# Four of the second layer's six conditioning vectors formed by VectorE sums during the first mixer, and the softmax reciprocals' products placed behind a score block's first transposes

## The chip, the cores and the metric

The kernel runs on one core of a Trainium2 chip, in float32. The metric is device time in microseconds of a whole execution. The kernel before took 1665.06 us in the median of three runs (1663.93 to 1668.5).

Engines are named as in the profile: PE (matrix products), DVE (vector), ACT (scalar, table functions), POOL (general), SP (issues DMAs). A queue is the list of DMAs that one engine issues in order.

## The reference

A two-layer backbone over 512 latent tokens and 256 context tokens, width 1024. Each layer: conditioning, a mixer, an expert layer. Layer 0 mixes by Fourier groups and a short gated convolution; layer 1 by windowed attention with four key heads. Cut to what the change touches:

```python
def reference(...):
    for layer in range(2):
        mod_l = silu(c) @ w_mod[layer] + b_mod[layer]        # 6 vectors of 1024, latent tokens
        mod_c = silu(c_ctx) @ w_mod[layer] + b_mod[layer]    # the same, context tokens
        sh1_l, sc1_l, g1_l, sh2_l, sc2_l, g2_l = split(mod_l, 6)
        sh1_c, sc1_c, g1_c, sh2_c, sc2_c, g2_c = split(mod_c, 6)
        hl = modulate(rms_norm(xl, norm_mix_g[layer]), sh1_l, sc1_l)   # vectors 0 and 1
        ...                                  # mixer; layer 1 makes no output for the context tokens
        xl = xl + g1_l * yl                                            # vector 2
        hl2 = modulate(rms_norm(xl, norm_ffn_g[layer]), sh2_l, sc2_l)  # vectors 3 and 4
        if last:
            xl = xl + g2_l * hier_moe(hl2, ...)                        # vector 5
```

In the last layer the context tokens need only vectors 0 and 1. In the attention, the weights of one query are exp(score - max) over their sum; the kernel multiplies by the reciprocal of that sum at the end.

## The kernel before, in words

**Stages.** Start and norm to 40 us; first mixer (input projection, four Fourier groups, four convolution groups) to 227; output projection and router of layer 0, `mixer_out`, to 326; experts of layer 0 to 830, which stream the experts' weights; keys, values and queries of layer 1 to 953; score blocks to 1100; `mixer_out` of layer 1 to 1157; experts of layer 1 to the end.

**Conditioning vectors.** `ModFeed` makes two vectors at a time (a group), for latent and context tokens at once, in four steps. A step takes a 2 MB piece of `w_mod` in a slot of a shared ring, multiplies it on PE by the silu of the conditioning (`sil`, 32 columns, eight float32 products of 512 columns, line 1035) and has DVE add the sum to the bias (line 1040); POOL stores the finished group in a scratch tensor in device memory, `mod_d` (line 1043). Groups 0 to 2 of layer 0 and group 0 of layer 1 are made in the first mixer: there the loads are issued by POOL (line 1013), each when PE has finished with the slot that it re-uses. Groups 1 and 2 of layer 1 are made in the attention layer, where SP issues the loads: two steps among the key and value blocks, one at the end of each of the first six score blocks.

**First mixer.** PE multiplies weights that are split into a high part (`whi`, by ACT) and a rest (`wlo`, by DVE, line 1206) by the normalized tokens: 24 pairs of a 512- and a 256-column product per group of 128 channels (lines 1210 and 1211). Four groups go through a discrete Fourier transform (lines 1227, 1250 and 1253, with DVE's butterflies into `Z` between), four through the convolution.

**Score blocks.** Eight blocks, each of eight heads by 128 queries. In block n PE makes the scores of block n, one or two heads at a time (line 1783; DVE adds the mask and finds the maximum, ACT takes exp, line 1789), and between them transposes the weights of block n-1 (`pv_tile`, line 1830) and multiplies them by the values (`pv_mm`, line 1845). At the end `pv_end` spreads the reciprocals `es` of block n-1 over the 64 rows of a head by 16 small products by the identity (line 1856), ACT copies them to SBUF (line 1858), DVE multiplies.

**What sets the order.** Outside stretches marked `in_order` a scheduler with a timeline of its own places the instructions of each engine; each engine then runs its list in that order and waits where a value is missing. PE's order in the score blocks and in `mixer_out` is the written one. SP's and POOL's queues run in their listed order too.

**mixer_out.** It needs the rows of `mod_d` that layer 0's group 1 and 2 hold: `md` (line 1325) for the router's products on PE (line 1331), `gr`, `a`, `h` and `b` (line 1337) for gates and norms. SP loads them all, after the six 512 KB tiles of `x` (line 1432), and before the experts' first weights `w` and `r` (line 721).

Of the kernel before, what the change touches and what calls it, by code (L numbers as in the profile page):

```python
# [10 lines left out]
F32 = mybir.dt.float32  # L11
# [9 lines left out]
D = 1024  # L21
# [64 lines left out]
def body(tc, I, out, upto=None, dbg=None):  # L86
# [29 lines left out]
    def close(*ps):  # L116
        for p in ps:
            p_close.pop(id(p)).__exit__(None, None, None)
# [23 lines left out]
    one_ = stat.tile([128, 1], BF, name="one_")  # L142
    V.memset(one_, 1.0)
    ones = one_.to_broadcast([128, 128])
    epst = stat.tile([128, 1], F32, name="epst")
    V.memset(epst, EPS)
    rsq = stat.tile([128, 2, 4], F32, name="rsq")
# [849 lines left out]
    class ModFeed:  # L997
# [20 lines left out]
        def step(self, again=-1):  # L1018
# [22 lines left out]
            if q == 3:  # L1041
                for s in range(2):
                    G.dma_start(mod_d[l, s, g * 2048:(g + 1) * 2048].rearrange("(q n) -> q n", q=4), bm[s:128:32, :])


    xsrc = [I["x"][0, m * 128:(m + 1) * 128, :] for m in range(4)] + [I["ctx"][0, m * 128:(m + 1) * 128, :] for m in range(2)]
    pp = pool("ps0", space=PSUM)
# [107 lines left out]
    def put_y(g, pieces):  # L1155
        if len(ym) == 2:
            ym.append(R1a.tile([128, 2, 8, 256], F32R, name="r2"))
        for i, v in enumerate(pieces):
            S.copy(ym[i][:, 0, g, :], v)
            V.tensor_sub(ym[i][:, 1, g, :], v, ym[i][:, 0, g, :].bitcast(F32))  # L1160

    tp = pool("ptmp")
    cw = tp.tile([128, 3, 4], F32, name="cw")
    for t in range(3):
# [55 lines left out]
    def four_b(g, aT):  # L1220

        U = fp.tile([128, 6, 256], F32, name="U")
        for mm in range(3):
            p = psB([128, 2, 256])
            for i in range(2):
                m = 2 * mm + i
                T.matmul(p[:, i, :], aT[:, m * 128:(m + 1) * 128], dch, start=True, stop=True)
            S.copy(U[:, 2 * mm:2 * mm + 2, :], p)
        sm = U[:, 0:2, :]
        df = fp.tile([128, 2, 256], F32, name="df")  # L1230
        Z = fp.tile([128, 6, 2, 128], F32, name="Z")
        V.tensor_sub(df, U[:, 0:2, :], U[:, 2:4, :])
        V.tensor_add(sm, U[:, 0:2, :], U[:, 2:4, :])

        def zf(e):
            return Z[:, e].rearrange("p a c -> p (a c)")

        V.tensor_add(zf(0), sm[:, 0], sm[:, 1])
        V.tensor_sub(zf(2), sm[:, 0], sm[:, 1])
        C0, S0, C1, S1 = df[:, 0, 0:128], df[:, 0, 128:], df[:, 1, 0:128], df[:, 1, 128:]  # L1240
        V.tensor_sub(Z[:, 1, 0], C0, S1)
        V.tensor_add(Z[:, 1, 1], S0, C1)
        V.tensor_add(Z[:, 3, 0], C0, S1)
        V.tensor_sub(Z[:, 3, 1], S0, C1)
# [12 lines left out]
    load_conv(0)  # L1257
    pre = proj_pre()
    for g in range(4):
        aT = four_a(g)  # L1260
        if g:
            with tc.issue_after(mm["last"].ins):
                feed.step()
        if prev is not None:
            four_b(g - 1, prev)
        feed.step()
        prev = aT
    wo = I["w_out_even"][0].rearrange("(j p) d -> p j d", p=128)

# [7 lines left out]
    for j in range(4):  # L1277
# [10 lines left out]
        csb = tp.tile([128, L + LC + 4], F32, name="t3", bufs=2)  # L1288
        S.copy(csb[:, 0:L + LC], pc)
        feed.step()  # L1290
        load_conv(j + 1)
        if j == 3:
            wout = load_wout(0, 1)
# [5 lines left out]
        V.scalar_tensor_tensor(z[:, 1:1 + N2], u[:, 0:N2], cw[:, 0, j:j + 1], z[:, 1:1 + N2], op0=ALU.mult, op1=ALU.add)  # L1299
        V.scalar_tensor_tensor(z[:, 1:1 + N2], u[:, 2:2 + N2], cw[:, 2, j:j + 1], z[:, 1:1 + N2], op0=ALU.mult, op1=ALU.add)  # L1300
        feed.step()
        pb = proj(lambda k0: wr4[:, k0:k0 + 4, 0, :])
# [4 lines left out]
    close(cp, tp, hp)  # L1307


    def mixer_out(layer, NT, lhs, raws, whl, x1, psA, psB, hq, rq, mk_route, h2dst, mdp):  # L1310
# [256 lines left out]
    def cps(shape):  # L1567
        return mps.tile(shape, F32, name="cp", bufs=2)
# [14 lines left out]
    run(rest0)  # L1583

    feed = ModFeed([(1, 1), (1, 2)], lambda: cps([128, 512]), False)
    feed.load(0)
    close(mps, R1b, R1a, mp)
    pp = pool("ps1", space=PSUM)  # L1590
    kvp = pool("kvp")
# [111 lines left out]
            S.copy(kS[part][0:64, :, ms], p)  # L1703
            (V.tensor_copy)(kS[part][64:128, :, ms], p)

    feed.psum_tile = lambda: psB([128, 512])
    raw0 = load_qkv(0, 3)
    for i in range(8):
        if i == 4:
# [3 lines left out]
        for f, d in ((st_norm, 0), (st_kv, 1), (st_kt, 3)):  # L1713
            if 0 <= i - d < (4 if f is st_kt else 6):
                f(i - d)
        if i == 0:
            feed.step()
        if i == 2:
            feed.step(None)
    close(cb)  # L1720

    qS = []
# [79 lines left out]

    ohi, olo = [hpl.tile([128, 8, L], F32R, name=n) for n in ("hhi", "hlo")]
    av = slot(1, [128, 8, 512])
    feed.load(2)
    def s_end(n):
        G_ = n // 4
        nm, ls = st_[n][1:3]
# [39 lines left out]
    def pv_end(n):  # L1848

        G_, b = divmod(n, 4)  # L1850
        po, es = st_[n][3:5]
# [5 lines left out]
        o = av[:, 4 + n % 2]  # L1857
        S.copy(o, p.rearrange("p i q -> p (i q)"))
# [7 lines left out]
    with in_order(mybir.EngineType.PE):  # L1866
        for n in range(1, 9):
            if n < 8:
                s_begin(n)
            for i in range(5):  # L1870
# [2 lines left out]
                    s_head(n, c)  # L1873
                if n == 1 and i < 2:
                    st_qt(1, 2 + i)
                if n > 0:
                    pv_tile(n - 1, i)
                    pv_mm(n - 1, i - 1)
            if n > 0:
                pv_mm(n - 1, 4)  # L1880
                pv_end(n - 1)
            if n < 7:
                feed.step()
            if n < 8:
                s_end(n)
    close(wp, ro, ap_, kvp, fdp)
# [72 lines left out]
```

## Time and profile before

| | |
|---|---|
| median of three runs | 1665.06 us (1663.93 to 1668.5) |
| profiled execution, its own time | 1659.86 us |
| span of its trace | 1658.0 us |
| PE busy | 1530.3 us, 92% of the span |
| DVE, ACT, POOL busy | 723.6, 440.3, 124.4 us |
| device memory read | 499.31 MB |

The span is the time from the first to the last instruction that the trace holds; the execution's own time is 1.86 us longer. The profile lists busy time per engine, a table of stretches, the chain of work that ended last, and, for each engine, what ended its idle times. An engine's idle time matters only where that chain passes through it.

### The profile page before, as it was taken

What the parts mean: (1) busy time and instruction counts of PE and PEld (TensorE: products, weight loads), DVE (VectorE), ACT (ScalarE), POOL (GpSimd) and SP (SyncE); (2) the same over time, 40 slices, a digit from 0 to 9 for tenths busy, and PEclk for the clock granted to TensorE, in tenths of its full rate; (3) what the DMA queues carried; (4) which work ended last, traced back from release to release, by engine and by line L of the source; (5) the groups of instructions that cost most, each with busy time, mean ns of one, the idle gap of its engine ahead of it and who ended that gap; (6) DMA issues with size and microseconds to landing.
All of it is one profiled execution on the core that took longest, in us unless ns stands there. A gap on an engine that the chain in (4) does not pass through costs nothing.

```text
span 1658.0 us, 21618 instructions
## 1 busy us (share of the span) xinstructions
PE 1530.3 (92%) x8123; PEld 863.6 (52%) x8123; DVE 723.6 (44%) x1638; ACT 440.3 (27%) x879; POOL 124.4 (8%) x128
## 2 busy tenths in 40 slices
PE   5999989889999999999989989899899999976887
PEld 3677878734444444434447865678444445431332
DVE  3532435963425343433468965546522323310223
ACT  4321212211111011111065665544322222210110
POOL 2520001300000000000032300000000000000000
PEclk9999999989999999999999999999899999998999
DMA  9775353879999999999931024372699999999996
GB/s 372 277 294 169 111 180 108 288 303 419 419 419 402 383 420 418 419 419 419 359 137 51 1 102 154 112 174 95 271 419 421 419 420 420 420 420 420 420 420 252
DMA packets 106399, 503.53 MB, mean 304 GB/s; under 512 B 18384, under 2 KB 33232, under 8 KB 52272
## 3 DMA queue, kind: packets, MB, share of 16 engines
q1 hardware_dynamic: 95776, 464.09, 70.8%
q0 software_dynamic: 7344, 34.81, 5.5%
q10 hardware_dynamic: 3168, 3.17, 0.6%
q8 instruction: 67, 1.10, 0.3%
q14 instruction: 44, 0.36, 0.1%
HBM read 499.31 MB, written 5.34 MB: 304 GB/s over the span
## 4 chain that ended last, share of the span: by engine, by line
PE 34%; DMA 10%; DVE 3%; ACT 3%; issue 1%; SPq 0%; ACTq 0%; DVEq 0%
PE p L860 9%; DMA hhi<-in_w_dram 5%; PE yp L931 5%; DMA w<-in_w_dram 4%; PE cp L809 3%; PE A L1378 3%; PE tp L765 3%; PE A L1660 2%; PE A L1783 2%; PE O L1845 2%; PE B L1830 2%; DMA r<-in_w_dram 1%; PE B L1035 1%; ACT P L1789 1%; PE tp L772 1%
## 5 line engine op out<-in xcount | busy, mean ns | idle before, releaser
L860 PE MATMUL p<-w,xt 128*64 128x512 f32 (+1 forms) x1024 | 339.5, 618 | 16.7 <-DMA w<-in_w_dram 16.6
L860 PE MATMUL p<-r,xt 128*64 128x512 f32 (+1 forms) x784 | 282.6, 611 | 10.2 <-DMA r<-in_w_dram 9.7
L810 DVE TENSOR_TENSOR x<-x,cp 128x512 f32<-128x512 f32 x224 | 147.8, 685 | 96.0 <-PE cp L809 95.8
L873 DVE TENSOR_TENSOR sg<-sg,p 128x512 f32<-128x512 f32 x29 | 20.0, 688 | 372.8 <-PE p L860 361.4
L809 PE MATMUL cp<-y,ot 128*128 128x512 f32 x616 | 172.2, 414 | 8.8 <-DVE x L810 4.9
L860 PEld LDWEIGHTS p<-w,xt 128*64 128x64 f32 (+1 forms) x1024 | 100.4, 136 | 135.3 <-issue 100.7
L931 PE MATMUL yp<-w,ht 128*64 128x512 f32 (+1 forms) x512 | 159.4, 595 | 4.3 <-DMA w<-in_w_dram 4.3
L860 PEld LDWEIGHTS p<-r,xt 128*64 128x64 f32 (+1 forms) x784 | 84.1, 136 | 143.8 <-issue 122.3
L809 PEld LDWEIGHTS cp<-y,ot 128*128 128x128 f32 x616 | 105.8, 189 | 51.6 <-DVE x L810 26.1
L931 PE MATMUL yp<-r,ht 128*64 128x512 f32 (+1 forms) x368 | 128.6, 595 | 0.7 <-ACT ht L892 0.7
L797 ACT CAST y<-yp 128x512 fp32r<-128x512 f32 x58 | 34.0, 585 | 278.6 <-DVE yp L793 185.6
L1378 PE MATMUL A<-r,r 128*128 128x512 f32 x288 | 71.1, 404 | 3.8 <-ACT r L1344 2.4
L931 PEld LDWEIGHTS yp<-r,ht 128*64 128x64 f32 (+1 forms) x368 | 38.1, 134 | 66.0 <-issue 63.9
L931 PEld LDWEIGHTS yp<-w,ht 128*64 128x64 f32 (+1 forms) x512 | 46.5, 131 | 48.6 <-issue 40.4
L860 PE MATMUL p<-hhi,xt 128*64 128x512 f32 (+1 forms) x128 | 62.0, 637 | 8.2 <-DMA hhi<-in_w_dram 8.2
L1378 PEld LDWEIGHTS A<-r,r 128*128 128x128 f32 x288 | 54.8, 194 | 15.7 <-ACT r L1344 2.7
L1787 DVE CUSTOM_DVE_ANT_0 A<-A,band,nsink 128x640 f32<-128x640 f32 (+1 forms) x56 | 45.1, 832 | 35.4 <-PE A L1783 35.4
L863 ACT ACTIVATE sg<-p 128x512 f32<-128x512 f32 x29 | 17.3, 597 | 156.7 <-PE p L860 156.7
L799 DVE TENSOR_TENSOR y<-yp,y 128x512 fp32r<-128x512 f32 x58 | 40.1, 691 | 40.0 <-ACT y L797 40.0
L860 PE MATMUL p<-hlo,xt 128*64 128x512 f32 (+1 forms) x112 | 54.9, 641 | 0.0
L1783 PEld LDWEIGHTS A<-kS,w 128*128 128x128 f32 x288 | 36.2, 188 | 32.5 <-ACT P L1789 14.8
L795 DVE SCALAR_TENSOR_TENSOR yp<-yp,gs,grow 128x512 f32<-128x512 f32 x26 | 19.7, 759 | 74.6 <-PE yp L931 74.6
(428 smaller groups left out, 2534.5 us busy)
## 6 DMA issues: line engine op xcount, KB each, us to landing
w<-in_w_dram SPq DMA_DIRECT2D x191, 1024.0 KB, 19.8
r<-in_w_dram SPq DMA_DIRECT2D x143, 1024.0 KB, 19.8
w<-in_w_mod_dram POOLq DMA_DIRECT2D x12, 2048.0 KB, 8.5
hhi<-in_w_dram SPq DMA_DIRECT2D x23, 1024.0 KB, 19.8
hlo<-in_w_dram SPq DMA_DIRECT2D x23, 1024.0 KB, 19.8
w<-in_w_mod_dram SPq DMA_DIRECT2D x11, 2048.0 KB, 8.8
w<-in_w_in_even_dram SPq DMA_DIRECT2D x13, 512.0 KB, 7.7
w<-in_w_out_even_dram SPq DMA_DIRECT2D x2, 2048.0 KB, 8.1
```

Source lines behind the costliest of these rows:

```text
L765: T.matmul(p, oh[:, m, :], near["h2"][m][i][:, hf * 512:hf * 512 + 512], start=n == 0, stop=n == 7)
L797: hi = S.copy(Yr[j, hf][0], ys)
L799: V.tensor_sub(Yr[j, hf][1], ys, Yr[j, hf][0].bitcast(F32))
L809: T.matmul(p, OT[j][:, m * 128:(m + 1) * 128], Yr[j, hf][i], start=n == 0 and i == 0, stop=n == len(js) - 1 and i == 1)
L810: return V.tensor_add(xs, xs, p)
L860: T.matmul(ps[rs], X[b][:, q, rs], W[j, wn, ab][:, q, :], start=q == 0, stop=q == 7)
L931: T.matmul(py_[hf][rs, :], HT[b][:, q % 4, rs], W[j, "w2", ab][:, q % 4, hf * 512:hf * 512 + 512], start=q % 4 == 0, stop=q % 4 == 3)
L1378: T.matmul(ps, lhs(m, a, j), whl[b][:, j, :], start=j == 0 and i == 0, stop=j == 7 and i == 2)
L1660: T.matmul(ps, h[st][:, k, ms], whl[k][b], start=k == 0 and i == 0, stop=k == 7 and i == 2)
L1783: T.matmul(ps[:, o0:o0 + w], qS[G_][:, c, b * 128:(b + 1) * 128], kS[part][:, 2 * G_ + c // 4, k0:k0 + w], start=part == 0, stop=part == 1)
L1787: V.tensor_tensor_reduce(out=ps[:, 0:w], in0=ps[:, 0:w], in1=bnd, op0=ALU.add, op1=ALU.min, scale=1.0, scalar=nsink[:, hd:hd + 1], accum_o ...
L1830: T.transpose(p[:, i, :], Ps[gl * 4 + i][:, t * 128:(t + 1) * 128], ident)
```

## The change

Three edits. `ModFeed` for groups 1 and 2 of layer 1 goes from the attention layer, with its eight steps. A new class `SumFeed` makes vectors 2 to 5 of layer 1, for latent tokens only, during the first mixer: 32 steps, each of which loads a 512 KB piece of `w_mod` by POOL's queue into one of two buffers (`mw`) and lets DVE multiply it by one column of `sil` and add it to a sum of 128 x 1024 (`acc`); after eight steps two products with a column of ones on PE add up the 128 partitions, DVE adds the bias to two rows, POOL stores them. To make room, the scratch tile `df` of the Fourier step now lies in a part of `Z`. And in the score blocks the sixteen products of the reciprocals, with ACT's copy, stand behind the block's first transposes in place of the block's end.

```diff
+    class SumFeed:
+        def __init__(self, layer, vectors, room):
+            self.acc = room.tile([128, D], F32, name="acc")
+            self.todo = [(v, k) for v in vectors for k in range(8)]
...
+        def tile(self):
+            return self.room.tile([128, D], F32, name="mw", bufs=2)
+        def load(self):
...
+                self.w.append(self.tile())
+                G.dma_start(self.w[-1], I["w_mod"][self.layer].rearrange("(p k) n -> p k n", k=8)[:, k, v * D:(v + 1) * D])
+        def step(self):
...
+            if k:
+                V.scalar_tensor_tensor(self.acc, w, sil[:, k, 0:1], self.acc, op0=ALU.mult, op1=ALU.add)
+            else:
+                V.tensor_scalar(self.acc, w, sil[:, k, 0:1], None, op0=ALU.mult)
+            if k == 7:
+                self.finish(v)
+            self.load()
+        def finish(self, v):
+            ps, b = psB([128, 512]), self.tile()
+            rows = b[0:64:32, 0:512]
+            G.dma_start(rows, I["b_mod"][self.layer, v * D:(v + 1) * D].rearrange("(q n) -> q n", q=2))
+            for r in (0, 32):
+                T.matmul(ps[r:r + 32, :], onef.to_broadcast([128, 32]), self.acc[:, r * 16:r * 16 + 512], start=True, stop=True)
+            for r in (0, 32):
+                V.tensor_add(b[r:r + 1, 0:512], ps[r:r + 1, :], b[r:r + 1, 0:512])
+            G.dma_start(mod_d[self.layer, 0, v * D:(v + 1) * D].rearrange("(q n) -> q n", q=2), rows)
...
-        df = fp.tile([128, 2, 256], F32, name="df")
         Z = fp.tile([128, 6, 2, 128], F32, name="Z")
+        df = Z[:, 4:6].rearrange("p e a c -> p (e a c)")
...
+    sums = SumFeed(1, (2, 3, 4, 5), sp)
     for g in range(4):
         aT = four_a(g)
         if g:
             with tc.issue_after(mm["last"].ins):
                 feed.step()
+        sums.step()
         if prev is not None:
             four_b(g - 1, prev)
         feed.step()
+        sums.step()
+        sums.step()
...
-    feed = ModFeed([(1, 1), (1, 2)], lambda: cps([128, 512]), False)
-    feed.load(0)
...
-        if i == 0:
-            feed.step()
-        if i == 2:
-            feed.step(None)
...
+    def pv_scale(n):
+        es = st_[n][4]
         p = psB([128, 4, 128])
         for i in range(4):
             for gl in range(2):
                 c = gl * 4 + i
                 T.matmul(p[gl * 64:gl * 64 + 64, i, :], es[:, c:c + 1].to_broadcast([128, 64]), ident, start=True, stop=True)
+        scale[n] = av[:, 4 + n % 2]
+        S.copy(scale[n], p.rearrange("p i q -> p (i q)"))
...
-                if n > 0:
-                    pv_tile(n - 1, i)
-                    pv_mm(n - 1, i - 1)
-            if n > 0:
-                pv_mm(n - 1, 4)
-                pv_end(n - 1)
-            if n < 7:
-                feed.step()
+                pv_tile(n - 1, i)
+                pv_mm(n - 1, i - 1)
+                if i == 0:
+                    pv_scale(n - 1)
+            pv_mm(n - 1, 4)
+            pv_end(n - 1)
```

In each of the four convolution groups `sums.step()` stands five times beside the three of `feed.step()`; 12 steps fall in the Fourier groups and 20 in the convolution.

In the listings below line numbers of after are higher: the Fourier and convolution products stand at 1259 and 1260, `ModFeed`'s products at 1037, its loads at 1015, `mixer_out`'s row loads at 1395 and 1383, the experts' weights at 723, the score products at 1833, transposes at 1880, value products at 1895, reciprocals' products at 1907.

PE, first mixer, in the Fourier groups, where `ModFeed`'s products of two 2 MB pieces (`w_` with its number) stand. Before, each is parted from the next by other products:

```order
L1035 MATMUL M<-w_560,sil 32x512 [waits DMASW2_49,DVE_49]
L1035 MATMUL M<-w_560,sil 32x512 x7
L1250 MATMUL A<-dl,Z 128x128 x7
L1253 MATMUL A<-dx,Z 128x128 x4
L1210 MATMUL A<-hhi_347,whi 128x512 [waits Activation_49]
```

After, two pieces and the first sum's products (L1088) follow each other:

```order
L1259 MATMUL A<-hhi_349,wlo 128x512
L1260 MATMUL A<-hhi_350,wlo 128x256
L1037 MATMUL M<-w_636,sil 32x512 [waits DMASW1_49]
L1037 MATMUL M<-w_636,sil 32x512 x7
L1037 MATMUL M<-w_717,sil 32x512 [waits DMASW5_49]
L1037 MATMUL M<-w_717,sil 32x512 x7
L1088 MATMUL B<-acc,onef 32x512 [waits DVE_49]
L1088 MATMUL B<-acc,onef 32x512
```

What moved: the products of `w_717` now stand straight behind those of `w_636`, and behind `w_579`'s by twelve pairs of 1259 and 1260 and `w_636`'s eight products; the slot of `w_717` is that of `w_579`.

SP, end of the first mixer, behind the six loads of `x`. Before, the router's rows came ahead of `a`, `h`, `b` and the experts' `w`:

```order
L1319 DMA gf<-in_norm_ffn_g_dram 128x8 [waits DMAHW1_49]
L1337 DMA gr<-mod_d 128x512 [waits DMAHW2_49,DMASW4_49]
L1325 DMA md_1795<-mod_d 128x2x8 [waits DMAHW3_49,DMASW4_49]
L1337 DMA gr<-mod_d 128x512 [waits DMAHW4_49,DMASW5_49]
L1325 DMA md_1921<-mod_d 128x2x8 [waits DMAHW5_49,DMASW5_49]
L1337 DMA a_2011<-mod_d 128x1024 [waits DMAHW6_49]
L1337 DMA gfr<-in_norm_ffn_g_dram 128x1024 [waits DMAHW7_49]
L1337 DMA h_2016<-mod_d 128x1024 [waits DMAHW0_49]
L1337 DMA b_2019<-mod_d 128x1024 [waits DMAHW1_49]
L721 DMA w_2572<-in_w_dram 128x2048 [waits DMAHW2_49,DVE_49]
```

After:

```order
L1395 DMA a_2142<-mod_d 128x1024 [waits DMAHW5_49,DMASW0_49]
L1395 DMA h_2147<-mod_d 128x1024 [waits DMAHW6_49,DMASW1_49]
L1395 DMA b_2150<-mod_d 128x1024 [waits DMAHW7_49]
L723 DMA w_2703<-in_w_dram 128x2048 [waits DMAHW0_49,DVE_49]
L1372 DMA wr<-in_w_router_g_dram 128x8x4 [waits DMAHW1_49,PE_49]
L1373 DMA wr<-in_w_router_e_dram 128x8x32 [waits DMAHW2_49]
L1374 DMA br<-in_b_router_g_dram 128x4 [waits DMAHW3_49]
L1375 DMA br<-in_b_router_e_dram 128x32 [waits DMAHW4_49]
L1377 DMA gf<-in_norm_ffn_g_dram 128x8 [waits DMAHW5_49]
L1395 DMA gr<-mod_d 128x512 [waits DMAHW6_49]
L1383 DMA md_1926<-mod_d 128x2x8 [waits DMASW5_49,DMASW4_49,DMASW6_49,DMASW3_49,DMASW7_49,DMASW2_49,DMAHW7_49,DMASW1_49,DMASW0_49]
```

What moved: three loads of 512 KB and one of 1 MB now stand ahead of the router's rows and of both `md`.

PE, a score block, where the block's end meets the next block's first heads (`O` the values' product, `es` the reciprocals, `kS` the keys). Before:

```order
L1845 MATMUL O<-w_7094,v_5923 64x512 [waits Activation_49] x2
L1856 MATMUL B<-cst,es 64x128 [waits PE_49]
L1856 MATMUL B<-cst,es 64x128 x7
L1035 MATMUL B<-w_7287,sil 32x512 [waits DMAHW6_49,PE_49]
L1035 MATMUL B<-w_7287,sil 32x512 x7
L1783 MATMUL A<-kS_5919,w_6481 128x256
```

After, in the next block, where its first two heads are done:

```order
L1833 MATMUL A<-kS_6049,w_6586 128x128
L1880 MATMUL B<-cst,P 128x128 x4
L1880 MATMUL B<-cst,P 128x128 [waits PE_49]
L1880 MATMUL B<-cst,P 128x128 x3
L1907 MATMUL B<-cst,es 64x128 [waits DVE_49,PE_49]
L1907 MATMUL B<-cst,es 64x128 x7
L1833 MATMUL A<-kS_6048,w_6586 128x256 [waits Activation_49]
```

What moved: at the block's end the reciprocals' and `ModFeed`'s products are gone, and the reciprocals' products stand between its first transposes and its next head, where that head waits for ACT.

## Rows read from the trace of the kernel before

**Rows 1.** The page: PE's busy time over the span, PE weight loads, others.

```profile
PE 1530.3 (92%) x8123; PEld 863.6 (52%) x8123; DVE 723.6 (44%) x1638; ACT 440.3 (27%) x879; POOL 124.4 (8%) x128
```

**Rows 2.** Stretches: busy us of PE, PEld, DVE, ACT, POOL; clock; DMA share; GB/s.

```profile
80.00:100.00 20.00, 20.00 (x137) 13.71 (x136) 5.29 (x11) 4.32 (x9) 3.83 (x6) 1.00 0.83 298
...
140.00:160.00 20.00, 20.00 (x124) 14.69 (x123) 5.68 (x11) 4.20 (x8) 0.00 (x0) 1.00 0.29 110
...
240.00:260.00 20.00, 16.07 (x68) 12.95 (x67) 7.61 (x13) 0.00 (x0) 0.00 (x0) 0.83 0.71 237
...
400.00:500.00 100.00, 99.72 (x470) 43.70 (x468) 33.10 (x54) 12.55 (x22) 3.96 (x4) 1.00 1.01 419
```

**Rows 3.** The chain that ended last, attention layer: start, us, what.

```profile
849.78 3.31 PE B L1035 x16
...
865.20 1.90 PE B L1035 x16
...
902.99 8.27 DMA w<-in_w_qkv_dram
...
977.12 1.85 PE B L1035 x16
...
1071.22 1.14 PE B L1856 x14
1072.36 1.85 PE B L1035 x16
```

**Rows 4.** PE's waits, 820 to 1190 us: total, times, longest.

```profile
PE A L1783 <- ACT P L1789: 9.5, 10, 1.7
```

**Rows 5.** Timeline of PE, second score block: start, us, instructions, [idle before].

```profile
982.49 0.91 PE L1783 MATMUL A<-kS,w 128*128 128x256 f32 x6 [1.08 <-ACT P L1789]
```

**Rows 6.** ModFeed's loads by POOL, 55 to 170 us: ns min/median/max; us to landing.

```profile
L1013 POOL DMA_DIRECT2D w<-in_w_mod_dram x10: 713/738/760, 61.8 to 138.3; - x10
...
DMA to landing us min/median/max: 7.7/8.2/10.7
```

**Rows 7.** Timeline of PE in the first mixer.

```profile
80.18 0.40 PE L1210 MATMUL A<-hlo,whi 128*128 128x512 f32 x1
...
80.54 0.40 PE L1210 MATMUL A<-hhi,wlo 128*128 128x512 f32 x1
...
81.22 1.92 PE L1035 MATMUL M<-w,sil 128*32 128x512 f32 x16
```

**Rows 8.** DMA issues, 0 to 300 us: KB each, median us from issue to landing.

```profile
x<-in_x_dram SPq DMA_DIRECT2D x4, 512.0 KB, 4.8
...
x<-in_ctx_dram SPq DMA_DIRECT2D x2, 512.0 KB, 8.4
```

**Rows 9.** DVE's groups by line, 0 to 330 us: busy us, mean ns; idle before.

```profile
L1206 DVE TENSOR_TENSOR wlo<-w,whi 128x512 fp32r<-128x512 f32 x28 | 19.2, 690 | 64.7 <-ACT whi L1204 64.7
L216 DVE SCALAR_TENSOR_TENSOR h<-h,rq,b 128x1024 f32<-128x1024 f32 x6 | 7.7, 1285 | 0.6
...
L1087 DVE TENSOR_SCALAR xt<-xt,rq 128x1024 f32<-128x1024 f32 x6 | 4.3, 751 | 0.1
L1361 DVE SCALAR_TENSOR_TENSOR a<-a,gfr 128x1024 f32<-128x1024 f32 x1 | 1.2, 1226 | 1.3 <-DMA gfr<-in_norm_ffn_g_dram 1.3
```

**Rows 10.** Timeline of PE at the start of the first output projection.

```profile
229.34 11.16 PE L1378 MATMUL A<-r,r 128*128 128x512 f32 x48 [2.35 <-ACT r L1344]
242.50 1.97 PE L1331 MATMUL B<-wr,md 128*128 128x36 f32 x16 [1.99 <-DMA md<-mod_d]
244.96 0.59 PE L1331 MATMUL B<-wr,md 128*128 128x36 f32 x2 [0.49 <-DMA md<-mod_d]
246.99 13.46 PE L1378 MATMUL A<-r,r 128*128 128x512 f32 x48 [1.44 <-DVE x L1383]
```

**Rows 11.** Timeline of SP's queue, same place.

```profile
240.42 0.38 SPq L1325 DMA_DIRECT2D md<-mod_d  x1
...
243.87 10.27 SPq L721 DMA_DIRECT2D w<-in_w_dram  x2
```

More of the change, by code (lines that the diff above doesn't have):

```diff
@@ L144, in body @@
     ones = one_.to_broadcast([128, 128])
+    onef = stat.tile([128, 1], F32, name="onef")
+    V.memset(onef, 1.0)
     epst = stat.tile([128, 1], F32, name="epst")
@@ L1043, in step @@
                     G.dma_start(mod_d[l, s, g * 2048:(g + 1) * 2048].rearrange("(q n) -> q n", q=4), bm[s:128:32, :])
+    class SumFeed:
+        def __init__(self, layer, vectors, room):
+            self.layer, self.vectors, self.room = layer, vectors, room
+            self.acc = room.tile([128, D], F32, name="acc")
+            self.todo = [(v, k) for v in vectors for k in range(8)]
+            self.w = []
+            self.ld = 0
+            for _ in range(2):
+                self.load()
+        def tile(self):
+            return self.room.tile([128, D], F32, name="mw", bufs=2)
+        def load(self):
+            if self.ld < len(self.todo):
+                v, k = self.todo[self.ld]
+                self.ld += 1
+                self.w.append(self.tile())
+                G.dma_start(self.w[-1], I["w_mod"][self.layer].rearrange("(p k) n -> p k n", k=8)[:, k, v * D:(v + 1) * D])
+        def step(self):
+            v, k = self.todo.pop(0)
+            self.ld -= 1
+            w = self.w.pop(0)
+            if k:
[4 more added lines that the diff above has]
+                self.finish(v)
+            self.load()
+        def finish(self, v):
[7 more added lines that the diff above has]
+            G.dma_start(mod_d[self.layer, 0, v * D:(v + 1) * D].rearrange("(q n) -> q n", q=2), rows)
     xsrc = [I["x"][0, m * 128:(m + 1) * 128, :] for m in range(4)] + [I["ctx"][0, m * 128:(m + 1) * 128, :] for m in range(2)]
@@ L1160, in put_y @@
             V.tensor_sub(ym[i][:, 1, g, :], v, ym[i][:, 0, g, :].bitcast(F32))
+    sp = pool("sp", side="right")
     tp = pool("ptmp")
@@ L1229, in four_b @@
         sm = U[:, 0:2, :]
-        df = fp.tile([128, 2, 256], F32, name="df")
         Z = fp.tile([128, 6, 2, 128], F32, name="Z")
+        df = Z[:, 4:6].rearrange("p e a c -> p e (a c)")
         V.tensor_sub(df, U[:, 0:2, :], U[:, 2:4, :])
@@ L1290, in body @@
         feed.step()
+        sums.step()
         load_conv(j + 1)
@@ L1301, in body @@
         feed.step()
+        sums.step()
+        sums.step()
         pb = proj(lambda k0: wr4[:, k0:k0 + 4, 0, :])
@@ L1306, in body @@
         feed.step()
-    close(cp, tp, hp)
+        sums.step()
+        sums.step()
+    close(cp, tp, sp, hp)
     def mixer_out(layer, NT, lhs, raws, whl, x1, psA, psB, hq, rq, mk_route, h2dst, mdp):
@@ L1704, in st_kt @@
             (V.tensor_copy)(kS[part][64:128, :, ms], p)
-    feed.psum_tile = lambda: psB([128, 512])
     raw0 = load_qkv(0, 3)
@@ L1804, in body @@
     av = slot(1, [128, 8, 512])
-    feed.load(2)
     def s_end(n):
@@ L1846, in pv_mm @@
                      start=t == 0, stop=t == nk - 1)
-    def pv_end(n):
-        G_, b = divmod(n, 4)
-        po, es = st_[n][3:5]
+    scale = {}
+    def pv_scale(n):
+        es = st_[n][4]
         p = psB([128, 4, 128])
@@ L1856, in pv_end @@
                 T.matmul(p[gl * 64:gl * 64 + 64, i, :], es[:, c:c + 1].to_broadcast([128, 64]), ident, start=True, stop=True)
-        o = av[:, 4 + n % 2]
-        S.copy(o, p.rearrange("p i q -> p (i q)"))
+        scale[n] = av[:, 4 + n % 2]
+        S.copy(scale[n], p.rearrange("p i q -> p (i q)"))
+    def pv_end(n):
+        G_, b = divmod(n, 4)
+        po, o = st_[n][3], scale[n]
         V.tensor_mul(o, o, po)
```

## The prediction, made before the changed kernel ran

> **What bounds the kernel now.** I read the totals first: PE is busy for 92% of the span [rows 1]. An average hides the stages, so next the stretches: in the first mixer PE is busy for all of each 20 us while DVE works for five and the DMA engines for 0.29 to 0.83 [rows 2]. There PE is the limit, and whatever is put on PE, or makes it wait, lengthens the stage. In the experts (400 to 500 us) both are full: 419 GB/s, a DMA share of 1.01, PE 99.72 of 100 us [rows 2]. This stage neither makes good a late start nor loses an early one, since its weights start with the router's end; I pass a delay of the mixer on at one for one, and likewise a gain of the attention layer.
>
> For the attention layer I read the chain that ended last. It runs through `ModFeed`'s products (line 1035): 3.31 and 1.90 us among keys and values, then six pieces of 1.85, the first and last of which are shown, each at the end of a score block, and before them the reciprocals' products (line 1856), 1.14 us for 14 of the 16 [rows 3]. Last, PE's waits: scores (line 1783) waited ten times for ACT's exp, 9.5 us in all [rows 4]; one such wait is 1.08 us, before the second heads of a block [rows 5].
>
> **What goes from the attention layer.** The six pieces at the blocks' ends: 6 x 1.85 = -11.1 us, since nothing but PE's own work stands between them and the chain. This is the firm term.
>
> The first two pieces, 3.31 + 1.90 = 5.2 us, are on the chain too, but behind them it passes through an 8.27 us load of `w_qkv` at 902.99 [rows 3]. A load that waits for a slot and not for PE comes no earlier, so I count -0.5; the ends are 0 and -5.2.
>
> The reciprocals' products are moved, not removed: 7 blocks x 1.14 = 8 us. Where they were, they delayed the next scores. Where they are now, the engine was waiting for ACT anyway [rows 4, 5]. If each fills a gap of its own size I gain up to 7.9; if ACT's exps set the pace of a block, the gap comes back elsewhere and I gain 0. Of the 9.5 us of waits most stand at these places, so I take -5.5.
>
> The added wait there is for DVE's reciprocals `es`; behind it on PE stand the next head's scores. `es` is formed at the end of the block before, two heads and a transpose earlier, so I cost it at nothing; if it were late, each 0.5 us would cost 7 x 0.5 = 3.5 us. The eight bias additions on DVE and the SP loads that vanish were beside other work: 0. Sum for this layer: -11.1 - 0.5 - 5.5 = -17.1 us, between -11 and -21.
>
> **What comes into the first mixer: PE.** A vector's finish is two float32 products of 512 columns. A `ModFeed` step has eight such in 1.92 us, four abreast [rows 7]; two abreast have half of the overlap each for half of the depth, an estimate of 0.93 us. Four finishes are 3.7; the last one falls into the 2.35 us in which PE waits for ACT before the output projection [rows 10]. I take +2.8, between 0 and 3.7.
>
> **PE waits for `ModFeed`'s pieces.** This is a matter of order. `w_717` can be loaded only when `w_579`'s products are done, and now PE comes to it after twelve pairs of products and `w_636`'s. From the starts 80.18 and 80.54 a pair takes 0.36 us [rows 7], so this is 12 x 0.36 + 1.9 = 6.2 us of work. A load takes 7.7 to 10.7 us to land, median 8.2, and its issue 0.74 [rows 6]; it stands in POOL's queue behind one `mw` load which waits for a sum. With 8.2 + 0.7 + 0.5 for that, PE waits 3.2 us; by the shortest and longest load 2 to 5.5. `w_773`, one finish and a few products further on, I cost at 0.6. Nothing else in the listing is nearer than 8 us. Together +3.9, between 0 (should the queue run ahead of what I think) and +10.
>
> **DVE.** 28 sums at 1.23 to 1.28 us and four at 0.75 [rows 9] are 38 us, and the eight small additions little more. DVE has the room: it works a quarter to a half of the stage and sat idle for 64.7 us before the splits alone, waiting for ACT [rows 9]. But its list is strict: a sum whose load has not landed holds the `wlo` split behind it, and PE's next pairs wait for that. While loads land in time, I count +1.5 for single collisions, and up to +8.
>
> Traffic: 32 x 512 KB = 16.8 MB more in about 157 us is 107 GB/s; 298 GB/s and 107 together are 405, just under the 419 at which the experts' stage stands [rows 2]. So the early Fourier groups have no room to catch up.
>
> **The router's rows.** On SP three loads of 512 KB and one of 1 MB now stand ahead of `md`: 2.62 MB / 419 GB/s = 6.3 us. Before, PE waited there 1.99 us for `md`, then 0.49 and 1.44 [rows 10]. Now both `md` are asked for at once, so PE waits some 2.0 + 6.3 = 8.3 in place of 3.9: +4.3. It is 0 if the loads of `x` ahead of all of these set the pace, and +10.3 if SP holds as long at the `w` load as it did in the row of 243.87 [rows 11].
>
> Mixer: 2.8 + 3.9 + 1.5 + 4.3 = +12.5 us, between +5 and +22.
>
> **The clock.** At 240 to 260 the granted clock was 0.83 [rows 2], part of it at the lower level, 1.2 GHz in place of 2.4: 48 products of line 1378 took 13.46 us, where 48 before them took 11.16 [rows 10]. Such a stretch costs 2.3 us. PE had worked without a gap for over 150 us and then had waits of 2.35, 1.99, 0.49 and 1.44. New waits in the mixer or a longer one at `md` may add a stretch, at even odds: +1.3, between 0 and 4.6.
>
> **Sum.** -17.1 + 12.5 + 1.3 = -3.3 us. The profiled execution took 1659.86 us, 1.86 more than its span; the shown median, 1665.06, is 5.2 above it. On the median's scale I forecast 1665.06 - 3.3 = 1662 us.
>
> **Rivals.**
>
> *The mixer hides it.* PE's pieces and `md` come in time, and only the finishes and a little of DVE cost, +3. For it: DVE's idle time and a POOL queue that is nearly empty. Against it: the listing leaves 6.2 us for a load of 8.2. Then -17.1 + 3 = -14, 1651 us.
>
> *The sums starve, the other side.* Two `mw` buffers serve 32 pieces and four bias rows: 36 turns, each a load and a sum of 1.23, two abreast. The time there is about 157 us: from 61.8 [rows 6] to the start of the last 24 pairs, 227 - 24 x 0.36 = 218. Two abreast this allows 157 x 2 / 36 = 8.7 us a turn, so a load may take 7.5. The same 512 KB took 4.8 us from `x` and 8.4 from `ctx` [rows 8]. At 4.8 nothing waits. At 8.4 the last sum is 36 x 9.6 / 2 - 157 = 16 us late, and in-order DVE hands most of it, 12, to PE: -3.3 + 12 = +8.7, 1674 us. It decides at 7.5 us.
>
> The Trainium skill has a rule that makes this worse: "SBUF — State Buffer", "SBUF: two separate sides", says that DMAs issued by POOL get no descriptors written while a VectorE instruction holds the port pair that both share; by its "Who interferes with whom" `tensor_scalar` can hold that pair, while for two-input sums only reads by POOL collide. Here the POOL issues took 0.71 to 0.76 us among DVE's two-input splits [rows 6, 9], which agrees. By this rule only the four `tensor_scalar` sums hold a load back, 4 x 0.75 = 3 us at most; if all 32 did, the turns would lengthen by 1.2 and the starving would set in at 6.3 us.
>
> *ACT sets the blocks' pace.* The reciprocals' products gain nothing, because the exps, and the copy that ACT now does earlier, fill a block anyway. For it: the waits on ACT recur block after block [rows 4]. Against: PE is busy in most of these blocks. Then -11.6 + 12.5 + 1.3 = +2.2, 1667 us.
>
> **Chances.** A measurement of this kernel can tell about 0.3%, 5 us, from no change. My forecast 0.47 (of it faster 0.15, within 0.29, slower 0.03); the mixer hides it 0.23, all faster; starving 0.18, all slower; ACT's pace 0.12 (within 0.09, slower 0.03). That makes faster 0.38, same 0.38, slower 0.24. The forecast's own range, from the partial bounds, is 1655 to 1669. The range for 8 in 10 takes in the hidden mixer at 1651 and starving up to its price: 1650 to 1674.
>
> **What would show it.** In the profile after: line 1037 gone from 840 to 1100 us, and line 1907 between transposes and scores, with waits for ACT down from 9.5 to about 4; the attention layer 17 us shorter. In the mixer: one idle time of PE of some 3 us before a `ModFeed` piece, with POOL's load issued under 7 us before it; PE waiting for `md` some 8 us in one piece; the output projection starting 6 to 10 us later than 229. I am wrong if PE's idle time before 227 is under 2 us or above 15, if PE waits for `wlo` behind a sum in more than a few places, or if the blocks shorten by 1.85 each and no more.

## The result, and the profile after

The changed kernel took 1655.94 us in the median of six runs (1652.73 to 1658.67), the kernel before 1664.49 in six: a ratio of 0.9947, 95% interval 0.9933 to 0.996. That is 8.5 us faster, where the forecast was 1662 and -3.3 us. The direction and the range held; the size did not. The runs below show that the parts of the change came to about nothing together, and that the gain came from a place of which the forecast had no term: the direction held by luck.

The profiled execution took 1657.86 us, its span is 1655.9. The page of after, busy time over the span (to [rows 1]):

```profile
PE 1525.1 (92%) x8011; PEld 866.5 (52%) x8011; DVE 759.7 (46%) x1671; ACT 440.3 (27%) x879; POOL 141.7 (9%) x160
```

DVE has 36 us more, the sums; PE only 5 less. In the first mixer, PE's waits of after, 40 to 340 us (total, times, longest):

```profile
PE B L1389 <- DMA md<-mod_d: 9.0, 1, 9.0
PE M L1037 <- DMA w<-in_w_mod_dram: 3.4, 1, 3.4
...
PE A L1299 <- DVE Z L1287: 1.5, 1, 1.5
...
PE B L1088 <- DVE acc L1075: 0.8, 1, 0.8
```

The first two are the two waits that were forecast, 8.3 us for `md` and 3.2 for `w_717`. Where PE waits for `w_717`, in the timelines of PE and of POOL:

```profile
104.44 1.92 PE L1037 MATMUL M<-w,sil 128*32 128x512 f32 x16 [3.40 <-DMA w<-in_w_mod_dram]
107.14 1.05 PE L1088 MATMUL B<-acc,onef 128*32 128x512 f32 x4 [0.77 <-DVE acc L1075]
```

```profile
95.15 0.75 POOL L1015 DMA_DIRECT2D w<-in_w_mod_dram  x1 [6.62 <-PE M L1037]
```

POOL's load ended its own wait with PE's products, not with a sum: the distance to the slot's last use was too short, and the queue was free. PE's next step began 9.3 us after the load was issued. The loads of this line now take longer to land than in [rows 6], in the median 9.8 us in place of 8.2; the second line is that of `mw`:

```profile
DMA to landing us min/median/max: 8.6/9.8/11.8
```

```profile
DMA to landing us min/median/max: 3.8/5.2/12.6
```

At 5.2 us the two `mw` buffers keep up: DVE's sums waited 16 times for a load, 24.9 us in all, but PE waited for a sum only the 0.8 us above. The rival of starving sums did not come. A finish costs 1.05 us, where I took 0.93.

At the output projection, PE's timeline of after (to [rows 10]), then SP's:

```profile
236.07 1.19 PE L1436 MATMUL A<-r,r 128*128 128x512 f32 x4 [1.37 <-ACT r L1402]
238.09 10.27 PE L1436 MATMUL A<-r,r 128*128 128x512 f32 x44 [0.83 <-DVE r L1403]
257.36 7.01 PE L1389 MATMUL B<-wr,md 128*128 128x36 f32 x32 [9.00 <-DMA md<-mod_d]
264.18 11.04 PE L1436 MATMUL A<-r,r 128*128 128x512 f32 x36
```

```profile
242.28 0.33 SPq L723 DMA_DIRECT2D w<-in_w_dram  x1
...
244.07 8.57 SPq L1374 DMA_DIRECT2D br<-in_b_router_g_dram  x1
...
255.33 0.43 SPq L1383 DMA_DIRECT2D md<-mod_d  x1
```

One wait of 9.00 in place of 1.99, 0.49 and 1.44; SP stands for 8.57 us at a small row behind the large ones. After the wait the 32 router products took 7.01 us, where 16 took 1.97 before, and PE ran at the lower level of its clock there (granted clock 0.50, 254 to 261 us):

```profile
254.00:261.00 7.00, 3.64 (x18) 3.67 (x18) 3.57 (x9) 0.00 (x0) 0.00 (x0) 0.50 0.87 223
```

In the score blocks the waits for exp, 9.5 us in [rows 4], are down to 1.9 (after, PE's waits, 973 to 1100 us):

```profile
PE A L1833 <- ACT P L1839: 1.9, 5, 0.5
PE B L1907 <- ACT w L1883: 1.9, 1, 1.9
```

The second line is new: once, the reciprocals' products waited 1.9 us for ACT.

What no term of the forecast spoke of stands in the stretches of the two expert stages. After, to the row of 400 to 500 us in [rows 2], and the second stage:

```profile
400.00:500.00 100.00, 99.83 (x467) 42.74 (x466) 41.25 (x66) 11.61 (x21) 2.97 (x3) 1.00 1.01 424
1250.00:1350.00 100.00, 100.00 (x475) 49.00 (x472) 31.04 (x50) 23.17 (x48) 0.00 (x0) 1.00 1.01 426
```

Before, second stage:

```profile
1250.00:1350.00 100.00, 100.00 (x477) 50.40 (x475) 32.33 (x52) 24.11 (x51) 0.00 (x0) 1.00 1.01 420
```

The DMA engines are as busy before as after (a share of 1.01 in each row), and yet move 424 and 426 GB/s in place of 419 and 420.

### The profile page after: what moved, and what is told of

It is laid out like the page before. It is cut to its first block, busy times and chain, and to the rows that moved or that the text cites. A ratio compares the mean times of both kernels' runs of the same rounds, so it can differ in the third digit from the quotient of the medians.

```text
span 1655.9 us, 21500 instructions
## 1 busy us (share of the span) xinstructions
PE 1525.1 (92%) x8011; PEld 866.5 (52%) x8011; DVE 759.7 (46%) x1671; ACT 440.3 (27%) x879; POOL 141.7 (9%) x160
## 4 chain that ended last, share of the span: by engine, by line
PE 34%; DMA 10%; DVE 3%; ACT 2%; issue 1%; SPq 0%; DVEq 0%; ACTq 0%
PE p L862 8%; PE yp L933 5%; DMA w<-in_w_dram 5%; DMA hhi<-in_w_dram 4%; PE A L1715 3%; PE cp L811 3%; PE A L1436 3%; PE tp L767 2%; PE A L1833 2%; PE O L1895 2%; PE B L1880 2%; ACT P L1839 1%; PE tp L774 1%; DVE x L812 1%; DMA w<-in_w_qkv_dram 0%
## 5 line engine op out<-in xcount | busy, mean ns | idle before, releaser
L862 PE MATMUL p<-w,xt 128*64 128x512 f32 (+1 forms) x1024 | 338.5, 611 | 14.3 <-DMA w<-in_w_dram 14.1
L862 PE MATMUL p<-hhi,xt 128*64 128x512 f32 (+1 forms) x128 | 66.0, 672 | 7.1 <-DMA hhi<-in_w_dram 7.1
L739 POOL DMA_INDIRECT r<-h_d,gi x17 | 17.0, 997 | 411.8 <-PE tp L774 342.4
```

Source lines behind the costliest of these rows:

```text
L862: T.matmul(ps[rs], X[b][:, q, rs], W[j, wn, ab][:, q, :], start=q == 0, stop=q == 7)
```

## The experiments

The stage table below is taken from the first and last start of one line of PE in each trace (output projection: line 1378 of before; values' products: 1845; experts of layer 0: from 860 to 931; experts of layer 1: from 860 to 809; lines of the others shifted). Times are us; "again" are second traces of before and after on one chip. The other columns are from other chips: on the three, the kernel before took 1663.71, 1662.86 ("+64 B", "md first") and 1665.22 us (last column). "md first" is SP's order of before, below.

| stage | before again | after again | after, slots +64 B | md first | md first, all at 256 |
|---|---|---|---|---|---|
| to the output projection's start | 228.2 | 237.3 | 240.1 | 237.9 | 238.3 |
| to the first experts' first product | 111.1 | 118.4 | 119.9 | 110.6 | 110.1 |
| experts of layer 0 | 488.9 | 485.9 | 488.8 | 484.7 | 484.9 |
| to the first value product | 139.5 | 141.3 | 142.2 | 138.5 | 132.8 |
| score blocks, and to line 1378 | 133.4 | 115.0 | 115.0 | 115.2 | 115.4 |
| output projection, router of layer 1 | 74.1 | 75.2 | 76.7 | 75.8 | 75.5 |
| experts of layer 1, last sums | 476.9 + 6.8 | 472.0 + 6.8 | 476.4 + 6.9 | 472.7 + 6.8 | 471.6 + 7.0 |
| span | 1658.9 | 1651.9 | 1666.0 | 1642.2 | 1635.6 |

**The kernel before, a second trace.**

> The kernel before, unchanged, for a second trace of it. In the two traces so far the experts of layer 0 took about 4 us less after the change and those of layer 1 about 2 us less, at 425 in place of 419 GB/s, though the change does not touch them. Theory (this is variation between executions): this trace differs from the first one of before by as much, and its whole time is the usual 1663 to 1668. Rival (the change makes the experts faster): this trace shows 419 GB/s again and the experts' stages as long as in the first, within 1 us.

1663.92 us, 1.0009 of before (0.9994 to 1.0023). Experts of layer 0 488.9 us (489.4 in the first trace), of layer 1 476.9 (476.8), at 419 and 420 GB/s. The theory fell: the difference is not one between executions. In the first traces of before and after it is 4.4 us in layer 0 and 4.9 in layer 1; the expectation had the latter too small.

**The changed kernel, a second trace.**

> The changed kernel, unchanged, for a second trace on the same chip as the other three. Theory: the first mixer to the end of the output projection again 15 to 16 us longer than before, PE waiting some 9 us for md and 3 us for one piece of w_mod, the score blocks 17 to 18 us shorter, keys/values/queries some 8 us longer; whole time 0.995 of before. Rival (the mixer's loss or that of keys/values/queries is an accident of one execution): one of these is under half of that here.

1655.68 us, 0.9953 (0.9934 to 0.9971). Each part came again: the first mixer and output projection 16 us longer, score blocks with the step to the projection 18.4 shorter, experts 3.0 and 4.9 shorter. Keys and values lost 4.0 us from their first product to their last, and 2.9 more up to the first value product (4.2 and 4.4 in the first trace), where 5.1 came free ahead of them, the first `ModFeed` piece among it.

**The reciprocals alone.**

`pv_end` is split into `pv_scale` and the rest as in the change; then:

```diff
...
+                    if i == 0:
+                        pv_scale(n - 1)
             if n > 0:
                 pv_mm(n - 1, 4)
                 pv_end(n - 1)
             if n < 7:
                 feed.step()
```

> The kernel before with one part of the change alone: the reciprocals' products and ACT's copy behind a block's first transposes; ModFeed as before. Theory (they fill PE's waits for ACT): waits of the scores for exp fall from 9.5 us to about 2, the score blocks get 6 to 8 us shorter, whole time -6 to -8 us, 0.996. Rival (ACT's exps set the pace of a block): waits stay above 6 us in sum, the whole time within 2 us of before.

1658.55 us, 0.9971 (0.996 to 0.9981), against 1663.71: -5.2. PE's waits, 960 to 1105 us, of this kernel:

```profile
PE A L1783 <- ACT P L1789: 2.1, 6, 0.4
PE B L1857 <- ACT w L1833: 1.6, 1, 1.6
```

The waits fell from 9.5 [rows 4] to 2.1, the blocks by 6.2 us; the first block's products, which now stand in front of the blocks, take 1.5 of it back. This is the theory, and my -5.5, though the whole time fell by less than the 6 to 8 us expected.

**The sums without the reciprocals.**

```diff
-                if i == 0:
-                    pv_scale(n - 1)
             pv_mm(n - 1, 4)
+            pv_scale(n - 1)
             pv_end(n - 1)
```

> The changed kernel with the other two parts alone: sums by VectorE in the first mixer and no ModFeed in the attention layer, but the reciprocals' products at a block's end as before. Theory: waits for exp in the score blocks come back to 8 to 10 us, the blocks are 11 us shorter than before in place of 17 to 18, whole time 6 to 8 us above the changed kernel and within 2 us of before; the stage of keys, values and queries stays as long as in the changed kernel but for the 3.5 us that the first block's products cost there. Rival (ACT's pace): as fast as the changed kernel.

1661.12 us, 0.998 (0.9968 to 0.9993): 5.4 above the changed kernel, where 6 to 8 were expected, and 2.6 below before. The reciprocals are worth as much here as alone (5.2), so the two parts add up. Waits for exp are back at 8.4 us, the blocks 10 us shorter than before.

**The column of ones alone.** The diff has a line that is not shown ahead: the column of ones for the finishes is a new tile, four bytes wide, in the first pool. It takes 32 bytes, and every weight slot that is allocated after it on that side lies 32 bytes further on.

```diff
+    onef = stat.tile([128, 1], F32, name="onef")
+    V.memset(onef, 1.0)
```

> The kernel before with nothing of the change but its four-byte column of ones, unused: every weight slot in SBUF lies 32 bytes further, from 32 bytes past a multiple of 64 to a multiple of 64 (the slots w0 to w3, and r0 and r1 of the second expert stage, from 224 past a multiple of 256 to a multiple of 256); the order of all instructions is that of before. Theory (where the slots lie sets the rate of the weights' DMAs): 424 GB/s in the first expert stage and 426 to 427 in the second, these 3 to 4 and 4.5 to 5 us shorter, whole time -7 to -9 us, and nothing else changed. Rival (the faster experts come from what the sums do to the queues): 419 GB/s and the time of before within 2 us.

1654.26 us, 0.994 (0.9919 to 0.996): -8.6 us, as much as the whole change, with every engine's instructions in the order of before. The experts take 485.8 and 472.2 us, 3.1 and 4.7 less than in the second trace of before. Its stretches:

```profile
400.00:500.00 100.00, 99.72 (x474) 43.17 (x472) 33.78 (x55) 12.38 (x22) 3.96 (x4) 1.00 1.01 425
...
1250.00:1350.00 100.00, 100.00 (x474) 50.24 (x473) 32.32 (x53) 24.78 (x53) 0.00 (x0) 1.00 1.01 427
```

**The changed kernel, slots 64 bytes further.**

```diff
     V.memset(onef, 1.0)
+    room64 = stat.tile([128, 16], F32, name="room64")
+    V.memset(room64, 0.0)
```

> The changed kernel with 64 bytes more ahead of the weight slots: all still at multiples of 64, w0 to w3 now 64 past a multiple of 256, no instruction moved. Theory A (multiples of 64 decide): 424 and 427 GB/s, time of the changed kernel within 2 us. Theory B (multiples of 256 decide): the rate falls back to 419 in the second expert stage, where all ring slots but two were at multiples of 256, and the time rises by 5 to 8 us.

1665.76 us, 1.0012 of before (1.0000 to 1.0025) and 10 us above the changed kernel. Its stretches:

```profile
400.00:500.00 100.00, 99.82 (x470) 44.52 (x468) 42.00 (x68) 12.53 (x22) 3.95 (x4) 1.00 1.01 420
1250.00:1350.00 100.00, 100.00 (x473) 46.33 (x470) 27.80 (x45) 21.97 (x46) 0.00 (x0) 1.00 1.01 421
```

Theory B: 256 decides, not 64. The rise is more than its 5 to 8 us: against the second trace of after the experts took 7.3 us more, and the other stages, in a trace 14.1 us longer, the rest; why those are longer stays open. The addresses in the built programs, as remainders by 256, beside the rates:

| | w0 to w3 | r slots, layer 0 | r0, r1, layer 1 | hhi, hlo | GB/s, layer 0 | layer 1 |
|---|---|---|---|---|---|---|
| before | 224 | 32 | 224 | 160 | 419 | 420 |
| after, +64 | 64 | 128 | 64 | 160 | 420 | 421 |
| after | 0 | 64 | 0 | 160 | 424 | 426 |
| all at 256 (below) | 0 | 0 | 0 | 0 | 426 | 427 |

The run shows the change without its accident, as near as it can be had: with the slots off a multiple of 256 as before, the moved work comes to +2.9 us (0 to 4). By the other way, the changed kernel at 0.9947 against the tile alone at 0.994, it comes to about 1. So it is worth nothing, or a small loss.

**SP's order of before.** The `a`, `gfr`, `h` and `b` rows and the experts' third weight load are issued after the router's rows and both `md`.

```diff
+            md_ins[layer] = Y.dma_start(md, mod_d[...]).ins
...
+                            with tc.issue_after(md_ins[layer]):
+                                a2 = row(hq, "a2", mod_d[layer, s, 4 * D:5 * D], E)
...
+                    if layer == 0 and len(issued) == 3:
+                        tc.add_manual_dep(issued[-1], md_ins[0].name, ...)
```

> The changed kernel with SP's order of before at the end of the first mixer: the router's rows and both md ahead of a, h, b and the experts' w. Theory (the bytes ahead of md make PE wait 9 us there, and the pause costs a stretch at the lower clock): PE waits under 3 us for md, the output projection's start to its end is back from about 95 to 89 us, whole time 6 to 9 us under the changed kernel. Rival (md comes late for another reason: it lies where the sums' buffers were and waits for the last store of the sums): PE still waits 5 us or more, whole time within 3 us of the changed kernel.

1644.55 us, 0.9893 (0.987 to 0.9915): 11 us under the changed kernel, more than the 6 to 9 expected. PE's timeline:

```profile
251.92 1.98 PE L1394 MATMUL B<-wr,md 128*128 128x36 f32 x16 [1.71 <-DMA md<-mod_d]
255.32 13.90 PE L1444 MATMUL A<-r,r 128*128 128x512 f32 x48 [1.43 <-DVE x L1449]
```

The wait is 1.71, so the bytes ahead of `md` were its cause; the rival (the last store of the sums) holds for no more than that. Output projection to experts: -7.8 us against the changed kernel. One stretch at the lower clock stays (13.90 for 48 products, as 13.46 in [rows 10]). A further 3 us came among keys and values, where PE's order also changed, since the scheduler made it anew; whether that order or the earlier start gave them was not taken apart.

**Two pieces back among keys and values.**

```diff
+    feed = ModFeed([(1, 1)], lambda: cps([128, 512]), False)
+    feed.load(0)
...
+        if i == 0:
+            feed.step()
+        if i == 2:
+            feed.step(None)
```

> The changed kernel with two ModFeed steps back among keys and values, as before the change; their sums are used by nothing. Theory (taking the two pieces out let PE's clock and the order of this stage slip, which ate what they cost): keys, values and queries up to the first value products back from 121 to 117 us or less though PE has 3.8 us more to do, whole time within 1 us of the changed kernel or below it. Rival (the pieces cost what they cost): whole time 3.5 to 5 us above the changed kernel.

1655.22 us, 0.9948 (0.9927 to 0.9968): the time of the changed kernel, with two more pieces on PE, and not the 3.5 to 5 us more of the rival. From the experts' end to the first value product it took 141.8 us with the pieces and 141.3 without; behind the first piece 117.7, just above the 117 that the theory allowed, in place of 120.6. PE behind its wait: in the second traces of before and of after, and in this kernel.

```profile
850.64 3.38 PE L1035 MATMUL B<-w,sil 128*32 128x512 f32 x16 [2.67 <-ACT r L1556]
853.95 2.11 PE L1660 MATMUL A<-w,hhi 128*128 128x512 f32 x8
```

```profile
862.25 3.78 PE L1715 MATMUL A<-w,hhi 128*128 128x512 f32 x8 [2.66 <-ACT r L1614]
865.83 3.07 PE L1715 MATMUL A<-w,hlo 128*128 128x512 f32 x8
```

```profile
862.04 3.64 PE L1037 MATMUL B<-w,sil 128*32 128x512 f32 x16 [2.66 <-ACT r L1614]
865.61 3.14 PE L1717 MATMUL A<-w,hhi 128*128 128x512 f32 x8
```

In these traces PE runs at the lower level of its clock around the wait (0.57 from 850 to 858 us and 0.71 from 858 to 866 in the second trace of after), and that falls on whatever PE does first behind it: a piece takes 3.4 to 3.6 there in place of 1.85 [rows 3], eight products 3.8 in place of 2.1. So the first piece paid in part with time that its successor pays now. That the rest is the order of this stage, which the scheduler makes anew in each kernel, is likely but not shown.

**Both repairs and the last slots.**

```diff
     sil = fdp.tile([128, 8, 32], F32, name="sil")
+    pad0 = fdp.tile([128, 48], F32, name="pad0")
+    G.memset(pad0, 0.0)
...
     lst = pool("lst", side="right")
+    pad1 = lst.tile([128, 40], F32, name="pad1")
+    G.memset(pad1, 0.0)
```

> The changed kernel with the router's rows and md ahead on SP, as in the run before it, and with 192 and 160 bytes of unused room that bring the remaining weight slots (four of layer 0's ring, two of layer 1's) to multiples of 256 too; no instruction of PE or SP is moved by it. Theory (a weight slot at a multiple of 256 is filled faster): 427 GB/s in the first expert stage in place of 424, 2 to 4 us less there, up to 1 us less in the second, whole time 1640 to 1643. Rival (the first stage is at its limit with PE at 99.8 of 100 us): the time of the run before, 1644.6, within 1.5 us.

1637.78 us, 0.9845 (0.9826 to 0.9864): the fastest, 27 us under before and 18 under the changed kernel. The rate is 426 and 427:

```profile
400.00:500.00 100.00, 99.72 (x474) 43.11 (x472) 37.13 (x60) 13.13 (x23) 3.95 (x4) 1.00 1.01 426
...
1250.00:1350.00 100.00, 100.00 (x476) 46.44 (x474) 28.66 (x47) 22.55 (x47) 0.00 (x0) 1.00 1.01 427
```

But the gain is not where the expectation put it, so its theory failed: the first experts took 484.9 us, as before the last shift (484.7), though the rate in this stretch rose from 424. This stage is not at the limit of its DMAs all through. From 500 to 600 us, in the kernel before and in the changed one:

```profile
500.00:600.00 100.00, 98.96 (x459) 44.66 (x457) 47.83 (x78) 11.41 (x20) 2.96 (x3) 1.00 0.97 398
```

```profile
500.00:600.00 100.00, 98.88 (x462) 45.03 (x460) 40.27 (x67) 12.51 (x22) 3.96 (x4) 1.00 0.95 394
```

There the DMA engines were not full, and moved less after than before. 5.7 us came behind the experts, up to the first value product, where PE's clock in this trace stayed at 1.00 from 842 to 858 us (0.50 and 0.71 without the shift). There PE's wait of 2.67 us was as long as in the traces above, and the eight products behind it took 2.11. Whether the shift is the cause of that, by the time at which the experts' last loads land, stays open; no instruction moved between the two kernels.

**Without the sums.** The kernel before, with the reciprocals moved and all slots at multiples of 256.

> The kernel before with the reciprocals' products moved and all weight slots at multiples of 256, and without the sums: ModFeed as before. Theory (the slots' place and the reciprocals are the change's whole gain, the sums' part alone comes to about nothing): 1664 - 5 - 9 - 3 = 1647, within 2 us, under the changed kernel's 1656. Rival (taking ModFeed out of the attention pays by itself): 1652 or more.

1645.51 us, 0.9891 (0.9869 to 0.9913), as the theory said; the rival's 1652 is out. The kernel without the sums is 10 us faster than the changed one, of which the rest of the slots gave 1 or 2 in the experts. It is 7.7 us slower than the run above, where the sums stand with SP's order mended. But by the traces 6.2 of these stand between the experts' end and the first value product (139.0 us here, 132.8 there), where the run above has its 5.7 us of open cause, and SP's order of before alone took 138.5. So with `md` in time the sums pay some 2 us that are accounted for; more is not shown.

## Why the prediction was right, and where it was wrong

The second traces of before and after, stage by stage, beside the forecast's terms:

| term | forecast | measured |
|---|---|---|
| first mixer: finishes, late pieces, DVE | 2.8 + 3.9 + 1.5 = +8.2 | +9.1 |
| `md` and the clock, up to the first experts | 4.3 + 1.3 = +5.6 | +7.3 |
| experts of layer 0 | 0 | -3.0 |
| attention layer | -17.1 | 256.3 - 272.9 = -16.6 |
| output projection and router of layer 1 | 0 | +1.1 |
| experts of layer 1 | 0 | -4.9 |
| sum | -3.3 | -7.0 |

**Right, and by its reasons:** the reciprocals' products (-5.5 forecast; -5.2 alone, -5.4 as the last part), the six pieces (-11.1 forecast; the blocks without the reciprocals' move 10 us shorter), PE's wait for `w_717` (3.2 forecast; 3.4 and 3.9 in the two traces, with no wait behind an `mw` load and a longer landing in its place), the sums that keep up with two buffers. The rival in which ACT sets the pace fell with the third run, that of starving sums with the landing times of `mw`, that of a hidden mixer with the waits. One reading in the rival of the starving sums was off: in the trace of before no POOL issue of [rows 6] ran beside a split of DVE. Some ran beside other two-input operations; the one at 138.34 us lay wholly within one and took 0.74 us. After, four issues of `mw` lay wholly within a two-input sum and took 0.53 to 0.55 us, as long as the median of all 32, 0.54, so these sums held no issue back.

**The step that failed** is the first: "This stage neither makes good a late start nor loses an early one". Delays were passed on one for one: the first experts took 484.7 and 485.9 us in two kernels in which they began 7 us apart. What failed is that the sum put the change of the stage's own length at nothing. It was read from rows in which the DMA engines are full, and it took the 419 GB/s there for a limit that no part of the change touches. A new tile of four bytes moved the slots which these DMAs fill. Two runs show it from both sides: the tile alone, with no instruction in another order, gives 0.994, and the changed kernel with its slots shifted off again gives 1.0012. Without that, the experts' two rows of the table are gone and the rest is +0.9 us: the forecast of -3.3 was 4 us too good, and its sign was right by luck. The range would have held either way.

**The sizes that were off** are in the mixer and behind it: `md` with its clock 1.7 us more, since the wait was 9.0 and 7.8 in the two traces against 8.3, and because the stretch at the lower clock also held the 32 router products, 7.01 us; the mixer 0.9 more, with finishes of 1.05 us. In the attention layer two misses nearly cancelled. The first pieces, forecast at -0.5, came to +1.8 up to the first value product: ahead of the keys 5.1 us came free, and behind that 6.9 were lost, of which some 1.5 are the first block's reciprocals. The score blocks and the step behind them, forecast at -11.1 - 5.5, came to -18.4. `es`, costed at nothing, held PE for 0.2 us in the second trace of after. The ranges given for the two sums, -11 to -21 and +5 to +22, are narrower than the ends of their parts, which come to -24 and to more than +30.

The part that the change is named for lost time as it stood: sums without the reciprocals took 1661.12 us, the tile alone 1654.26. By their ratios to before, 0.998 and 0.994, that is 0.4% or 7 us; by the whole change, 0.9947, less the reciprocals and the tile, it is 5 to 6. The order on SP's queue accounts for all of it: with that mended, the stretch up to the first experts was 7.8 us shorter, and the whole kernel 11.

## What to carry to other kernels

Where a stage is bound by DMA, read the addresses of its buffers before and after a change, even if no line of the diff names them: one small tile in an early pool moves all that follow. Where work is moved into a stage, read what it does to the queue of the next: small rows that an engine waits for belong ahead of large loads that are not needed yet. And take a change apart before crediting it: here one part gained 5 us, one lost 5 to 7, and an accident gained 9.

## What the runs showed of the hardware

The rate at which weights are filled into SBUF depends on where the slot begins: 419 to 421 GB/s with no slot at a multiple of 256 (remainders 32, 64, 128, 160 and 224), 424 and 425 with four of the eight slots of a stage there, 426 and 427 with six or all eight, each with the DMA engines at a share of 1.01. A remainder of 64 in place of 224 gained no more than 1 GB/s.

The Trainium skill, "DMA: Bandwidth & Descriptors", "How a descriptor splits into AXI transactions", says that a transaction starts at a multiple of 256 bytes, and that a piece which starts elsewhere costs beats for bytes that aren't used. It says so of what is read; here the source was the same in all runs and the place written to was moved, and the trace agrees in direction. By its account, an estimate: 8192 bytes from a multiple of 256 are 256 beats, from 224 behind one they are 263, 2.7%; measured were 420 and 427, 1.7%. From 64 behind one they are 258, 0.8%, by the same estimate; measured were 421 and 427, 1.4%. So the size of the remainder counted for less here than that account has it, and why the place written to matters stays open.

PE's clock behind an idle time. In the output projection PE's clock fell to the lower level (1.2 GHz) behind its waits and stayed there longer behind the long one. The changed kernel, 254 to 275 us (the first of these rows stands above), then before, 240 to 254 us, where the waits were 1.99, 0.49 and 1.44 us [rows 10]:

```profile
261.00:268.00 7.00, 7.00 (x25) 6.23 (x26) 2.48 (x4) 0.00 (x0) 0.00 (x0) 0.50 0.20 84
268.00:275.00 7.00, 7.00 (x28) 5.67 (x28) 1.39 (x2) 0.00 (x0) 0.00 (x0) 0.88 0.01 2
```

```profile
240.00:247.00 7.00, 3.08 (x22) 2.40 (x20) 2.62 (x7) 0.00 (x0) 0.00 (x0) 0.86 0.76 190
247.00:254.00 7.00, 7.00 (x21) 5.56 (x22) 3.60 (x5) 0.00 (x0) 0.00 (x0) 0.65 0.81 336
```

The clock column shows 0.50, 0.50 and 0.88 against 0.86 and 0.65. I had counted such a stretch as one price of 2.3 us.
